# A two-layer hybrid decoder step on one core: new places for gate sums, first products and index writes, and a last norm taken token by token inside the loop

## The chip, the core and the metric

The program runs on one core of a Trainium2 chip. The engines are TensorE (PE), VectorE (DVE), ScalarE (ACT) and GpSimd (POOL); SyncE (SP) issues most DMAs and POOL the rest. The metric is the device time of one execution in microseconds; three runs of the kernel before gave 2693.7, 2697.02 and 2700.03 us, median 2697.02 us.

## What is computed

One inference step for a group of 256 prompt tokens (with 16 meta tokens ahead of them) and a group of 8 x 4 sample tokens, in all 320 columns with padding, of width 1024:

```python
for i in range(DEPTH):                      # 2 layers
    xn = rms_norm(h, norm_mix[i])
    h = h + (rwkv7_time_mix(xn, ...) if i % 2 == 0 else mamba2_mix(xn, ...))
    h = h + peer_ffn(rms_norm(h, norm_ffn[i]), w_q, sub_keys, u_tab, v_tab)
return rms_norm(h, norm_final), states...

def peer_ffn(xn, w_q, sub_keys, u_tab, v_tab):
    q = (xn @ w_q).reshape(T, 8, 2, 128)
    s = einsum('thzd,zhkd->thzk', q, sub_keys)          # two half-keys, 128 each
    sv, si = top_k(s, 16)
    top_s, pos = top_k(all 16 x 16 sums of sv, 16)      # 16 experts of 16384, per head
    gate = softmax(top_s)
    act = gelu(einsum('td,ted->te', x, u_tab[eidx]))
    return einsum('te,ted->td', gate * act, v_tab[eidx])
```

## The kernel before, in words

The residual `h` lies feature-major: 128 partitions, 8 blocks, 320 token columns. Four stages run one after the other: `rwkv` (0 to 427 us in the profiled execution), `peer` of layer 0 with three groups of 16 gathered tokens (to 1354 us), `mamba` (to 1753 us), `peer` of layer 1 with two groups (to 2675 us), and then `final`. Every stage opens tile pools in SBUF and PSUM and closes them at its end. The two `peer` stages are blocks of their own, whose order on each engine is a planner's: it goes by its own estimate of when things are ready, takes what was written first among what is ready, and leaves an instruction marked with `keep_in_program_order` behind everything that was written before it on its engine. The order on the chip is then fixed, and each engine works through it strictly.

**Products in three parts.** `load_w` (L288) fetches a 512 KB weight block into `wraw` (three buffers, SP), rounds it into `whi` (ACT, or POOL where told, L273/L275) and puts the rest into `wlo` (DVE L280 or POOL L278), two buffers each. `mm3` (L294) multiplies: eight pairs whi x xhi, whi x xlo, then eight wlo x xhi, 24 matmuls.

**The norm ahead of a stage.** `prenorm` (L320) makes `xh`, `xl` from h times the norm's weight without the mean square; `rmsnorm` (L304) takes squares on ACT, sums groups of four on DVE, and has PE sum over partitions (`psn`, L313); then square root (ACT L315) and reciprocal (DVE L316). The first products use the unnormed xh, xl, and their result is multiplied by the reciprocal (L876, L1281, L1313). `xn` (L318) is made besides.

**`peer` in its stages.** 16 query products (L869 on) and 96 score matmuls `pss` (L900). Then the U loop: 56 chunks b, in each of which a 512 KB block of the U table is split (low part on POOL, `leng=LP`) and multiplied with the tokens (`psc`, L299 to L302), with a gelu on ACT. DVE meanwhile does the two-level top-k of three token tiles (0: the samples, 1 and 2: the prompt halves), step by step from `topk`. At fixed chunks (`AFTER`, L1056) come the late parts: `gates` (L987: exp on ACT, its place kept, then sum, reciprocal and product on DVE) and, for tile 0, `indices` (L1001: two DVE instructions, six small writes to DRAM and three reads back, all DMAs issued by POOL) or, for tiles 1 and 2, `finish` (L993: three PE transposes `ptk`, place kept, then a copy to `sel`). Tile 1: gates at chunk 29, finish at 33; tile 2: 46 and 51; tile 0: 14 and 16.

Then the W loop: 64 groups of four tokens; one-hot rows are made on POOL, DVE and ACT and multiplied into per-token weights (L1101), with ten more U chunks between. Then the V loop: 128 chunks, each with 12 matmuls `acc` (L1202) on a split block of the V table; between them the remaining 62 U chunks and, in the background from chunk 20 to `G1`, the gathered rows of the 16-token groups (POOL indirect DMAs, DVE products L1124). At its end the four `acc` banks (two token halves, two feature halves) are copied, transposed back (L1221) and added to h (L1224). `h` itself is parked in DRAM (`hd`) and read back at chunk 122 (L1186), since its SBUF room serves as a buffer.

**`mamba`** projects 41 weight blocks (`proj`, L1256): first block 40 in `decays`, then the convolution blocks 32, 36, 16 and on. `NU` = 2 products use the unnormed input; ahead of the third, xh and xl are written again from `xn`. The products have two PSUM banks.

**`final`** (L1571) runs the feature-major rmsnorm on h and stores y in one DMA.

Of the kernel before, what the change touches and what calls it, by code (L numbers as in the profile page):

```python
# [23 lines left out]
F32 = mybir.dt.float32  # L24
# [143 lines left out]
def prep(I):  # L168
# [21 lines left out]
    A["vecs"] = v  # L190
    for g in _GROUPS:
        A[g] = pack_consts(g)
# [32 lines left out]
class K:  # L225
    def __init__(self, ctx, tc, a, o):
# [3 lines left out]
        self.pst = self.wr = None  # L230
# [27 lines left out]
    def psum(self, **tags):  # L258

        if self.pst is not None:  # L260
            self.pst.close()
        self.pst = ExitStack()
        self.ps = self.pst.enter_context(self.tc.tile_pool(name="ps", bufs=1, space=PSUM))
        self.pstags = tags
# [17 lines left out]
    def fetch(self, src, kb=8):  # L282
        raw = (self.wr or self.wp).tile([128, kb, 128], F32, name="wraw", tag="wraw", bufs=3)
        self.nc.sync.dma_start(raw, src)
        return raw
# [18 lines left out]
    def rmsnorm(self, out, h, g, sq, rp, tag="ps", rr=None):  # L304
# [3 lines left out]
        for k in range(KB):  # L308
            nc.scalar.activation(sq[:, k], h[:, k], AF.Square)
            if k % 4:  # L310
                nc.vector.tensor_add(sq[:, k], sq[:, k], sq[:, k - 1])
            if k % 4 == 3:
                nc.tensor.matmul(ps, lhsT=self.C["ones"], rhs=sq[:, k], start=k == 3, stop=k == KB - 1)  # L313
        r, ri = rr or (rp.tile([128, T], F32, name=n, tag=n) for n in ("rms", "rmsi"))
# [5 lines left out]
    def prenorm(self, out, h, g, xh, xl, sq, rr, tag):  # L320

        nc = self.nc
        for k in range(KB):
            nc.scalar.activation(xh[:, k], h[:, k], AF.Copy, scale=self.vec(g, k))
            nc.vector.scalar_tensor_tensor(xl[:, k], h[:, k], self.vec(g, k), xh[:, k].bitcast(F32), op0=ALU.mult, op1=ALU.subtract)
        self.rmsnorm(out, h, g, sq, None, tag, rr)
# [3 lines left out]
    def rwkv(self):  # L330
# [5 lines left out]
        self.wr = st.enter_context(tc.tile_pool(name="wr", bufs=3))  # L336
        st2 = ExitStack()
        bq = st2.enter_context(tc.tile_pool(name="q10", bufs=6))
        self.wp = st2.enter_context(tc.tile_pool(name="w", bufs=2))
# [140 lines left out]
        self.wp = st2.enter_context(tc.tile_pool(name="wn", bufs=2))  # L480
# [45 lines left out]
        def load_wo(n):  # L526
            for m in range(len(wt), n):
# [4 lines left out]
                else:  # L532
                    hi = self.wp.tile([128, KB, 128], F32R, name="whi", tag="whi", bufs=4)
                    lo = self.wp.tile([128, KB, 128], F32R, name="wlo", tag="wlo", bufs=4)
# [27 lines left out]
        self.wp = st2.enter_context(tc.tile_pool(name="wd", bufs=2))  # L562
# [17 lines left out]
        self.wr = None  # L580
# [249 lines left out]
    def peer(self, l, ng):  # L830
# [14 lines left out]
        gp = st.enter_context(tc.tile_pool(name="gp", bufs=1))  # L845
        self.wp = st.enter_context(tc.tile_pool(name="w", bufs=2))
        tp = st.enter_context(tc.tile_pool(name="tk", bufs=1))
# [6 lines left out]
        self.consts("cp", gp)  # L854
# [12 lines left out]
        ri = self.prenorm(xn, self.h, f"nf{l}", xh, xl, sq, (gview(60, (128, T)), gview(62, (128, T))), "m")  # L867

        qT = gview(20, (128, 16, T)); sk = gview(40, (128, 16, 128))  # L869
        for i in range(16):  # L870
            w = self.load_w(a[f"wq{l}"][i], heng=nc.gpsimd if i < LH else None, leng=8 if i < LQ else None)
# [4 lines left out]
            V.tensor_mul(qT[:, i], pq, ri)  # L876
# [33 lines left out]
        def topk(ti):  # L910
# [90 lines left out]
            def indices():  # L1001
# [3 lines left out]
                for i in range(3):  # L1005
                    dst = scr_i[i] if i < 2 else scr_g
                    src = ei[:, i] if i < 2 else fl(ts)
                    for hh in range(2):
                        x = nc.gpsimd.dma_start(dst[:, 64 * hh:64 * hh + 64], src[64 * hh:64 * hh + 64])
                        if i + hh == 0:  # L1010
                            tc.keep_in_program_order(x)
                    nc.gpsimd.dma_start(gi[:, i] if i < 2 else gg, dst[0:48].rearrange("(g t) (h m) -> (t h) g m", g=3, m=16))

            late[ti] = (gates, finish if ti else indices)
# [613 lines left out]
```

## Time and profile before

| | |
|---|---|
| three runs, median | 2697.02 us (2693.7 to 2700.03) |
| the profiled execution's own time | 2695.28 us |
| its span, first to last instruction | 2693.5 us |
| PE busy | 2500.8 us, 93% of the span |
| DVE, ACT, POOL busy | 1880.4, 1257.7, 1013.1 us |
| mean granted clock of TensorE | 0.968 |
| DMA | 460.28 MB, mean 171 GB/s |

PE is busy nearly throughout, so what is left to gain or lose lies in the stretches where it is not, and in those in which the granted clock is below 1.00. The profile is read stage by stage: first the busy time by stretch, then what PE waited for, then the instructions in order of time around each such wait.

### The profile page before, as it was taken

The page shows a single profiled execution, that of the slowest core. Times are in us where ns is not written, and L with a number is a line of the kernel's source. Part 1 is how long each engine was busy: PE and PEld are TensorE (multiplying, and loading weights), DVE is VectorE, ACT ScalarE, POOL GpSimd, SP SyncE. Part 2 cuts the span into 40 slices and gives each one's busy share as a digit, 9 for nine tenths or more (in the row PEclk, how much of TensorE's full clock was granted, in tenths as well). Part 3 has the DMA queues.
Part 4 walks back from the last instruction along what each step waited for, and adds up shares of the span by engine and source line. Part 5 has one row for each costly group of instructions (what it writes and reads, how often), then busy time and mean ns, then how long its engine had stood idle before and what let it go on. Part 6 is the DMA issues. An engine that isn't in the chain of part 4 may idle for free. (4 is left out here: it accounts for less than half of the span.)

```text
span 2693.5 us, 47369 instructions
## 1 busy us (share of the span) xinstructions
PE 2500.8 (93%) x18261; PEld 2168.8 (81%) x18261; DVE 1880.4 (70%) x3692; ACT 1257.7 (47%) x2337; POOL 1013.1 (38%) x896
## 2 busy tenths in 40 slices
PE   7999998978999999999969898989789899999997
PEld 4677768978988888888855786989789788888885
DVE  5355556795595677778783787759938856777776
ACT  3322223434784444444556543335347744444443
POOL 4111110468880232424156445006678601223120
PEclk9999999989999999999989999999899999999998
DMA  3111114434416788888732443354353267888774
GB/s 147 52 45 50 34 59 157 137 121 147 141 56 208 248 313 302 301 301 313 245 99 86 145 160 116 126 175 148 113 155 111 73 219 250 272 270 271 259 268 143
DMA packets 125154, 460.28 MB, mean 171 GB/s; under 512 B 14688, under 2 KB 15616, under 8 KB 121600
## 3 DMA queue, kind: packets, MB, share of 16 engines
q1 hardware_dynamic: 98784, 360.69, 41.4%
q0 software_dynamic: 26144, 96.56, 10.0%
q8 instruction: 144, 2.36, 0.4%
q14 instruction: 82, 0.67, 0.1%
HBM read 440.38 MB, written 16.82 MB: 170 GB/s over the span
## 5 line engine op out<-in xcount | busy, mean ns | idle before, releaser
L273 ACT CAST whi<-wraw 128x1024 fp32r<-128x1024 f32 (+1 forms) x619 | 643.2, 1039 | 890.9 <-PE acc L1202 243.0
L280 DVE TENSOR_TENSOR wlo<-wraw,whi 128x1024 fp32r<-128x1024 f32 (+1 forms) x493 | 598.3, 1214 | 369.9 <-ACT whi L273 345.3
L299 PE MATMUL psc<-xh,whi 128*128 128x256 f32 x2048 | 516.5, 287 | 2.0 <-ACT whi L273 2.0
L300 PE MATMUL psc<-xl,whi 128*128 128x256 f32 x2048 | 517.2, 287 | 0.0
L278 POOL TENSOR_TENSOR wlo<-wraw,whi 128x1024 fp32r<-128x1024 f32 (+1 forms) x150 | 356.7, 2385 | 194.6 <-PE pq L302 92.2
L299 PEld LDWEIGHTS psc<-xh,whi 128*128 128x128 f32 x2048 | 392.3, 192 | 8.5 <-ACT whi L273 3.7
L300 PEld LDWEIGHTS psc<-xl,whi 128*128 128x128 f32 x2048 | 392.0, 191 | 5.3
L302 PE MATMUL psc<-xh,wlo 128*128 128x256 f32 x2048 | 299.5, 286 | 34.5 <-POOL wlo L278 34.5
L302 PEld LDWEIGHTS psc<-xh,wlo 128*128 128x128 f32 x2048 | 269.2, 191 | 36.0 <-POOL wlo L278 35.4
L1202 PE MATMUL acc<-whi,glo 128*128 128x512 f32 x1024 | 279.4, 394 | 6.7 <-DVE glo L280 6.7
L1202 PE MATMUL acc<-whi,gh 128*128 128x512 f32 x1024 | 280.1, 394 | 4.3 <-ACT whi L273 3.3
L1032 POOL DMA_INDIRECT G<-in_un,gi x80 | 110.1, 1377 | 457.2 <-DVE glo L280 316.4
L1202 PE MATMUL acc<-wlo,gh 128*128 128x512 f32 x1024 | 276.5, 392 | 0.9 <-DVE wlo L280 0.9
L1202 PEld LDWEIGHTS acc<-whi,glo 128*128 128x128 f32 x1024 | 193.2, 189 | 51.0 <-DVE glo L280 7.6
L1202 PEld LDWEIGHTS acc<-wlo,gh 128*128 128x128 f32 x1024 | 192.8, 189 | 44.4 <-DVE wlo L280 2.2
L1129 POOL DMA_INDIRECT G<-in_v,gi x80 | 120.4, 1505 | 278.3 <-DVE G L1124 166.1
L1202 PEld LDWEIGHTS acc<-whi,gh 128*128 128x128 f32 x1024 | 184.0, 189 | 40.0 <-ACT whi L273 6.4
L1101 PE MATMUL pwt<-ob,oa 128*128 128x128 f32 x1024 | 145.3, 280 | 9.5 <-DVE ob L1075 6.1
L1101 PEld LDWEIGHTS pwt<-ob,oa 128*128 128x128 f32 x1024 | 128.9, 191 | 18.3 <-issue 14.3
L299 PE MATMUL pi<-xh,whi 128*128 128x320 f32 x328 | 107.7, 340 | 10.3 <-DVE cst L1281 7.4
L280 DVE TENSOR_TENSOR glo<-G,gh 128x256 fp32r<-128x256 f32 x256 | 107.0, 419 | 3.1 <-ACT gh L273 3.1
L1083 POOL TENSOR_SCALAR oa<-cp,sel 128x128 f32<-128x128 f32 x128 | 105.7, 835 | 7.5 <-issue 4.3
(469 smaller groups left out, 4453.9 us busy)
## 6 DMA issues: line engine op xcount, KB each, us to landing
wraw<-in_u SPq DMA_DIRECT2D x256, 512.0 KB, 3.9
wraw<-in_v SPq DMA_DIRECT2D x256, 512.0 KB, 4.4
wraw<-in_win SPq DMA_DIRECT2D x41, 512.0 KB, 3.7
wraw<-in_wq SPq DMA_DIRECT2D x32, 512.0 KB, 4.1
wraw<-in_rkv SPq DMA_DIRECT2D x24, 512.0 KB, 3.4
h<-in_ssm SPq DMA_DIRECT2D x8, 1024.0 KB, 7.9
out_sssm<-h POOLq DMA_DIRECT2D x8, 1024.0 KB, 5.3
wraw<-in_wo SPq DMA_DIRECT2D x8, 512.0 KB, 4.6
```

Of the source, the lines that this page charges most:

```text
L273: self.nc.scalar.copy(hi, x)
L278: self.nc.gpsimd.tensor_sub(lo[:, :n], x[:, :n], hi[:, :n].bitcast(F32))
L280: self.nc.vector.tensor_sub(lo[:, n:], x[:, n:], hi[:, n:].bitcast(F32))
L299: nc.tensor.matmul(ps, lhsT=whi[:, k], rhs=xhi[:, x0 + k], start=start and k == 0, stop=False)
L300: nc.tensor.matmul(ps, lhsT=whi[:, k], rhs=xlo[:, x0 + k], start=False, stop=False)
L302: nc.tensor.matmul(ps, lhsT=wlo[:, k], rhs=xhi[:, x0 + k], start=False, stop=stop and k == kb - 1)
L1032: nc.gpsimd.indirect_dma_start(out=rows, out_offset=None, in_=a[f"un{l}"], in_offset=bass.IndirectOffsetOnAxis(ap=gi[:, 0, g, m:m + 1], ax ...
L1083: nc.gpsimd.tensor_scalar(oa[:, j], C["iota"], sel[:, 0, t:t + 1], None, op0=ALU.is_equal)
L1101: mm(pw[:, j], lhsT=oa[:, j], rhs=ob[:, j], start=True, stop=True)
L1129: nc.gpsimd.indirect_dma_start(out=rows, out_offset=None, in_=vrows, in_offset=bass.IndirectOffsetOnAxis(ap=gi[:, 1, g, m:m + 1], axis=0))
L1202: mm(acc[i], lhsT=g[:, t0:t0 + 128], rhs=w[:, d0:d0 + 512], start=b == 0 and g is gh and w is vhf, stop=b == 127 and w is vlf)
```

## The change

Pools of `peer` and `mamba` and all PSUM pools are opened with `reuse_waits="tile"`: a tile in reused room waits for the tiles whose bytes it takes, and no longer for the whole pool that lay there. The weight pool (`wraw`, `whi`, `wlo`) is opened once for the whole program; the first three weights of a stage are fetched ahead of its constants. In `prenorm` the first product is written between the squares and their sum on PE. Query products alternate between two PSUM tags, and the first four mamba products have two banks each of two tags and are all unnormed. Of the late parts exp, gate sums and finish or indices have three places now; the DVE sum keeps its place; all nine index DMAs keep their place on POOL, six writes first, then three reads, after chunk 55. In the last layer h is transposed to token-major inside the V loop and the last norm is taken there token by token; `final` is gone and y has 288 rows.

```diff
-        self.ps = ...tile_pool(name="ps", bufs=1, space=PSUM)
+        self.ps = ...tile_pool(name="ps", bufs=1, space=PSUM, reuse_waits="tile")
+        self.wp = ctx.enter_context(tc.tile_pool(name="w", bufs=2))      # in K.__init__
...
     def rmsnorm(self, out, h, g, sq, rp, tag="ps", rr=None, mid=None):
...
-            if k % 4 == 3:
+            if k % 4 == 3 and mid is None:
                 nc.tensor.matmul(ps, lhsT=self.C["ones"], rhs=sq[:, k], ...)
+        if mid is not None:
+            mid()
+            for k in (3, 7):
+                self.tc.keep_in_program_order(
+                    nc.tensor.matmul(ps, lhsT=self.C["ones"], rhs=sq[:, k], ...))
...
# peer
+        raws = {i: self.fetch(a[f"wq{l}"][i]) for i in range(3)}
-        gp = st.enter_context(tc.tile_pool(name="gp", bufs=1))
+        gp = st.enter_context(tc.tile_pool(name="gp", bufs=1, reuse_waits="tile"))
...
-        self.consts("cp", gp)
+        with tc.issue_after(self.fetched):
+            self.consts("cp", gp)
...
-            pq = self.bank([128, T], "pq", "s")
+            pq = self.bank([128, T], "pq", "so"[i % 2])
...
+            def exps():
+                tc.keep_in_program_order(nc.scalar.activation(es, es, AF.Exp))
             def gates():
-                tc.keep_in_program_order(nc.scalar.activation(es, es, AF.Exp))
-                V.tensor_reduce(mxs, es, axis=AX.X, op=ALU.add)
+                tc.keep_in_program_order(V.tensor_reduce(mxs, es, axis=AX.X, op=ALU.add))
...
-        AFTER = ((14, 16), (29, 33), (46, 51))
+        AFTER = ((14, 16, 55), (29, 31, 39), (46, 46, 52))
...
# peer, last layer: in the gather generator, for the ng groups of 16 tokens
+            if last:
+                for half in range(2):
+                    ph = self.bank([128, 512], "ph", "s")
+                    for g in range(ng):
+                        for k in range(4):
+                            mm(ph[32 * g:32 * g + 16, ...], lhsT=self.h[:, 4 * half + k, 16 * g:16 * g + 16], rhs=C["eye"], ...)
+                    for g in range(ng):
+                        nc.scalar.copy(o, ph[32 * g:32 * g + 16])
+                        V.tensor_add(o, o, ga[half][32 * g:32 * g + 16])
...
+        def normed(z, ps, i, rows):
+            for half in range(2):
+                V.scalar_tensor_tensor(yt half, z half, 1.0, z half, op0=mult, op1=mult, accum_out=f[:, half:half + 1])
+            V.tensor_add(f[:, 2:3], f[:, 0:1], f[:, 1:2])
+            nc.scalar.activation(f[:, 2:3], f[:, 2:3], AF.Sqrt, bias=C["cst"][ps, 0:1], scale=1.0 / D)
+            V.reciprocal(f[:, 3:4], f[:, 2:3])
+            for half in range(2):
+                V.scalar_tensor_tensor(yt[:, c], z[:, c], f[:, 3:4], gfin[ps, c], op0=ALU.mult, op1=ALU.mult)
+                nc.sync.dma_start(self.o["y"][rows, c], yt[:, c])
...
-        G1 = 120
+        G1 = 124 if last else 120
...
-            if b == 122:
+            if b == (120 if last else 122):
                 nc.sync.dma_start(self.h, hd)
+            if b == 124 and last:                       # 16 transposes of h, 4 copies on ACT
...
+        if last:                                        # after the loop, instead of L1211 to L1224 and final
+            for i in range(2):
+                for half in range(2):
+                    V.tensor_add(ht[i] half, ht[i] half, acc[2 * i + half])
+                normed(ht[i], slice(0, 128), 2 + i, slice(32 + 128 * i, 160 + 128 * i))
...
# mamba
+        raws = {b: self.fetch(a["win"][b]) for b in (40, 32, 36)}
-        NU = 2
+        NU = 4
+        pre = {b: self.load_w(a["win"][b], leng=LE, raw=raws[b]) for b in (40, 32)}
...
-            p = self.bank([128, T], "pi", "i")
+            p = self.bank([128, T], "pi", "i" if done[0] % NU < 2 or done[0] >= NU else "f")
...
-    def final(self): ...
```

## Rows read from the trace of the kernel before

**Rows 1.** Busy time of each engine in three stretches: the start of peer 0, the start of mamba, the V loop of peer 1. Columns: length, then busy us and instructions of PE, weight loads, DVE, ACT, POOL, then the granted TensorE clock, the DMA share and GB/s.

```profile
420.00:470.00 50.00, 41.53 (x258) 39.75 (x258) 30.34 (x44) 16.56 (x27) 5.54 (x4) 0.90 0.54 177
...
1350.00:1400.00 50.00, 34.27 (x196) 30.78 (x194) 44.81 (x65) 30.55 (x63) 25.73 (x31) 0.86 0.36 115
...
2140.00:2672.00 532.00, 529.09 (x2988) 462.87 (x2988) 367.25 (x479) 254.33 (x378) 99.08 (x67) 0.99 0.76 250
```

**Rows 2.** The waits of PE over the whole span, the three longest in total: who waited, for whom, us in total, times, longest.

```profile
PE psc L302 <- POOL wlo L278: 34.5, 4, 13.3
PE psn L313 <- issue: 27.3, 4, 9.7
PE ptk L996 <- DVE G L991: 20.2, 2, 10.1
```

**Rows 3.** The timeline from the last product of rwkv to the scores of peer 0: start, us, engine, line, operation, count, idle time before it in brackets.

```profile
426.70 0.45 PE L302 MATMUL po<-oh,wlo 128*128 128x320 f32 x2
...
434.80 1.41 PE L313 MATMUL psn<-G,c 128*128 128x320 f32 x2 [7.64 <-issue]
...
489.28 1.34 PE L302 MATMUL pq<-xh,wlo 128*128 128x320 f32 x8
492.80 1.34 PE L302 MATMUL pq<-xh,wlo 128*128 128x320 f32 x8
...
497.50 3.73 PE L900 MATMUL pss<-G 128*128 128x128 f32 x32
```

**Rows 4.** The same from mamba to peer 1.

```profile
1749.99 0.69 DVE L280 TENSOR_TENSOR wlo<-wraw,whi 128x512 fp32r<-128x512 f32 x1
...
1752.32 0.75 PE L302 MATMUL pout<-hl,wlo 128*128 128x320 f32 x4
...
1825.40 3.73 PE L900 MATMUL pss<-G 128*128 128x128 f32 x32
```

**Rows 5.** The same from peer 0 to the third product of mamba.

```profile
1354.83 3.73 ACT L324 ACTIVATE xh<-h,vecs 128x320 fp32r<-128x320 f32 x8 [1.21 <-PE pot L1221]
...
1361.25 2.88 PE L313 MATMUL psn<-sq,c 128*128 128x320 f32 x4 [6.80 <-issue]
...
1379.17 0.61 PE L299 MATMUL pi<-xh,whi 128*128 128x320 f32 x1 [7.39 <-DVE cst L1281]
```

**Rows 6.** Busy time in stretches of the U loop and the W loop of peer 0, columns as in the first group.

```profile
560.00:570.00 10.00, 9.48 (x80) 9.27 (x78) 10.00 (x61) 2.99 (x6) 3.67 (x2) 1.00 0.36 130
570.00:580.00 10.00, 0.00 (x0) 0.00 (x0) 10.00 (x54) 0.00 (x0) 0.76 (x2) 0.67 0.00 1
580.00:590.00 10.00, 7.24 (x44) 7.24 (x45) 10.00 (x31) 2.86 (x4) 5.77 (x4) 0.64 0.36 111
590.00:600.00 10.00, 6.04 (x31) 5.83 (x31) 10.00 (x31) 2.48 (x3) 9.84 (x9) 0.70 0.36 112
630.00:640.00 10.00, 1.72 (x15) 1.47 (x13) 9.90 (x7) 2.66 (x4) 4.79 (x3) 0.75 0.54 159
...
710.00:720.00 10.00, 10.00 (x90) 10.00 (x89) 10.00 (x24) 9.13 (x29) 9.27 (x12) 1.00 0.35 107
```

**Rows 7.** POOL's timeline in the U loop of peer 0.

```profile
537.09 2.39 POOL L278 TENSOR_TENSOR wlo<-wraw,whi 128x1024 fp32r<-128x1024 f32 x1 [0.49 <-ACT whi L273]
539.97 2.43 POOL L278 TENSOR_TENSOR wlo<-wraw,whi 128x1024 fp32r<-128x1024 f32 x1 [0.49 <-ACT whi L273]
...
579.24 1.10 POOL L1009 DMA_DIRECT2D scr_g<-G  x2 [15.56 <-DVE G L945]
...
584.98 0.81 POOL L1012 DMA_DIRECT2D gg<-scr_g  x1
590.12 2.11 POOL L1009 DMA_DIRECT2D scr_i<-ei  x4 [4.34 <-DVE ei L1004]
...
596.87 1.56 POOL L1012 DMA_DIRECT2D gi<-scr_i  x2
```

**Rows 8.** DVE's timeline at the end of the top-k of peer 0.

```profile
611.30 3.41 DVE L984 TENSOR_TENSOR G<-G 128x2048 bf16<-128x2048 bf16 x1
...
637.50 1.22 DVE L984 TENSOR_TENSOR G<-G 128x2048 bf16<-128x2048 bf16 x1
...
640.97 0.28 DVE L989 TENSOR_REDUCE G<-G 128x8 f32<-128x128 f32 x1
...
641.51 0.29 DVE L991 TENSOR_TENSOR G<-G 128x128 f32<-128x128 f32 x1
```

**Rows 9.** The timeline of the V loop's end and of what follows it.

```profile
2601.35 1.28 DVE L1124 SCALAR_TENSOR_TENSOR G<-G,act 128x1024 f32<-128x1024 f32 x1
...
2671.01 1.07 PE L1202 MATMUL acc<-wlo,gh 128*128 128x512 f32 x4
2672.07 1.09 PE L1221 MATMUL pot<-c,G 128*128 128x128 f32 x8
...
2687.96 0.34 SPq L1579 DMA_DIRECT2D out_y<-y  x1
```

**Rows 10.** DMA issues: KB of each, median us from issue to landing.

```profile
wraw<-in_wout SPq DMA_DIRECT2D x16, 256.0 KB, 2.9
...
h<-hd SPq DMA_DIRECT2D x2, 1280.0 KB, 7.8
...
out_y<-y SPq DMA_DIRECT2D x1, 1280.0 KB, 4.5
```

More of the change, by code (lines that the diff above doesn't have):

```diff
@@ L190, in prep @@
     A["vecs"] = v
+    A["nfin"] = np.ascontiguousarray(I["norm_final"].reshape(1, D))
     for g in _GROUPS:
@@ L262, in psum @@
         self.pst = ExitStack()
-        self.ps = self.pst.enter_context(self.tc.tile_pool(name="ps", bufs=1, space=PSUM))
+        self.ps = self.pst.enter_context(self.tc.tile_pool(name="ps", bufs=1, space=PSUM, reuse_waits="tile"))
         self.pstags = tags
@@ L282, in fetch @@
     def fetch(self, src, kb=8):
-        raw = (self.wr or self.wp).tile([128, kb, 128], F32, name="wraw", tag="wraw", bufs=3)
-        self.nc.sync.dma_start(raw, src)
+        raw = self.wp.tile([128, kb, 128], F32, name="wraw", tag="wraw", bufs=3)
+        self.fetched = self.nc.sync.dma_start(raw, src).ins
         return raw
@@ L1008, in indices @@
                     for hh in range(2):
[L1009 to L1014, printed above, removed]
+                        tc.keep_in_program_order(nc.gpsimd.dma_start(dst[:, 64 * hh:64 * hh + 64], src[64 * hh:64 * hh + 64]))
+                for i in range(3):
+                    tc.keep_in_program_order(
+                        nc.gpsimd.dma_start(gi[:, i] if i < 2 else gg,
+                                            (scr_i[i] if i < 2 else scr_g)[0:48].rearrange("(g t) (h m) -> (t h) g m", g=3, m=16)))
+            late[ti] = (exps, gates, finish if ti else indices)
         late_u = []
@@ L1062, in peer @@
             for ti in range(3):
-                for i in range(2):
+                for i in range(3):
                     if b == AFTER[ti][i]:
@@ L1209, in peer @@
             pass
+        if last:
+            for i in range(2):
+                for half in range(2):
+                    V.tensor_add(ht[i][:, half * 512:half * 512 + 512], ht[i][:, half * 512:half * 512 + 512], acc[2 * i + half])
+                normed(ht[i], slice(0, 128), 2 + i, slice(32 + 128 * i, 160 + 128 * i))
+            st.close()
+            return
         for i, pt in enumerate(self.gpt):
@@ L1232, in mamba @@
         st = ExitStack()
-        pp = st.enter_context(tc.tile_pool(name="mp", bufs=1))
-        self.consts("cm", pp)
+        raws = {b: self.fetch(a["win"][b]) for b in (40, 32, 36)}
+        pp = st.enter_context(tc.tile_pool(name="mp", bufs=1, reuse_waits="tile"))
+        with tc.issue_after(self.fetched):
+            self.consts("cm", pp)
         xh = pp.tile([128, KB, T], F32R, name="xh")
@@ L1269, in proj @@
             return p
-        gp = st.enter_context(tc.tile_pool(name="mg", bufs=2))
+        first = []
+        ri = self.prenorm(xn, self.h, "nm1", xh, xl, ep.tile([128, KB, T], F32, name="sq", tag="E"), (rr[:, 0], rr[:, 1]), "t",
+                          lambda: first.append(proj(40)))
+        gp = st.enter_context(tc.tile_pool(name="mg", bufs=2, reuse_waits="tile"))
         def conv(blk):
```

109 lines of the change are left out of this document (66 added, 43 removed).

## The prediction

> **What bounds the kernel now.** I read the busy time by stretch first. The V loop runs PE at 529.1 of 532 us [rows 1], and the U and W loops come near it, so nothing is won where PE runs at 1.00; the first reading also shows the exceptions: at a stage's start PE stands for a tenth to a third of 50 us, at a granted clock of 0.90 or 0.86 [rows 1]. Then I read PE's waits: three kinds make 82 us [rows 2], and each comes once per boundary or once per peer layer. psn waits at stage starts; psc waits for POOL's low parts in the U loop; ptk waits for DVE's gates. The timeline around each says why. "issue" is the name for a wait whose releaser is not seen; at psn it is the chain h, xh, squares, sums. Last I read the 21.4 us behind the last acc matmul (2672.08 to 2693.5) [rows 9]: one chain with PE nearly idle.
>
> **The change part by part.** The sum stands against the profiled execution, 2695.3 us (span 2693.5 and 1.8 around it), 1.7 under the median of 2697.0.
>
> *rwkv to peer 0.* From the last product (427.15) to the scores (497.50) pass 70.3 us [rows 3]. The PE work in it at full clock: 16 products at 3.52 (492.80 less 489.28) make 56.3; four psn matmuls, 1.41 per two at the low level [rows 3], half of that at the high one: 1.4; eight transposes at 0.14 (1.09 for eight [rows 9]): 1.1. That is 58.8, so 11.5 is waiting (7.64 [rows 3]) and half-speed running after it. Removed: the wait of every new tile for the whole old pool, and psn's place ahead of the first product. The weights can be fetched and split by POOL while rwkv ends; xh and xl follow h block by block; only block 7 is left when PE ends, one piece each on DVE, ACT and DVE again of some 0.47 us (3.73 for eight [rows 5]), and the first 14 matmuls (2.1 us at 3.52 for 24) cover it. Late next: psn's second half needs eight squares on ACT, which at no more than 0.47 each end about 4.7 us after the last product, against 3.5 of the first product: 1 us. I take -10.5; bounds -11.5 and 0 (if a tile under xh is read to the end).
>
> *mamba to peer 1.* 1753.07 to 1825.40 is 72.3 [rows 4], 13.5 over the same 58.8. Here the weight buffers come free only with mamba's last splits (1749.99 [rows 4]), so the first low part may be 1 to 2 us late. -11.5; bounds -13.5 and 0.
>
> *peer 0 to mamba.* xh starts at 1354.83 right behind the transposed h [rows 5], and no pool holds it; that stays. The 6.80 ahead of psn shrinks, since the first product follows xl at 0.47 per block; the 7.39 ahead of the third product [rows 5] shrinks, since four products instead of two run before xh, xl are rewritten. PE alone would be 11 us earlier. But DVE, which makes xl twice, xn and the convolutions, is busy 44.8 of these 50 us [rows 1] and does the same work. Its 5.2 idle us are the nearest limit: -6; bounds -11 and 0. The three constants that now queue on SP behind the weights, the exp and the mask copy put in their place, and the changed banks cost nothing while ACT and SP have room here (ACT 30.6 of 50); without it 1 or 2 us.
>
> *U loops, twice.* A chunk takes 2.88 us (539.97 less 537.09 [rows 7]). At 579 POOL stands 15.56 us in front of a small write, waiting for tile 0's gates, and 4.34 at 590 [rows 7]; the low parts of the next chunks are queued behind it, and PE idles 17.2 of the 40 us from 560 (0.5, 10, 2.8, 4.0) and runs another 13.3 at a granted clock of 0.64 to 0.70 [rows 6], a mix of the 1.2 and the 2.4 GHz level, which costs some 4.4: about 22 us. At chunk 55 those gates have been ready for 100 us, so this goes. What is late next is tile 1's gate sum: it stands at the very end of DVE's order, behind all of tile 2's top-k (640.97, done 641.8 [rows 8]), and DVE is busy 10.00 of 10 up to there [rows 6]. Keeping the sum's place only forbids an earlier one, so I cost it at nothing. PE came to the old finish, chunk 33, 10.1 before that [rows 2], at 631.7; 22 earlier and six chunks on (17.3) it comes to the new one at 627, so PE waits there longer than before. And DVE will end later: the same operation takes 1.22 us with POOL quiet and 3.41 with POOL subtracting [rows 8]. Some eleven such operations ran in POOL's pauses; each now pays 0 to 2.2: I take 6 in all (the middle of a uniform start would be 12, but after one wait the next ones run in the gap), bounds 0 and 24. DVE's release comes at 648; 16 chunks are then left where 22 were: -17.3 + 6 = -11.
>
> The Trainium skill, "SBUF — State Buffer", section "Who interferes with whom", says that GpSimd and a VectorE operation on the shared port pair exclude each other for the whole instruction. Taken at its worst here, eleven whole subtracts (2.39 each [rows 7]), DVE would end 26 us later, each U loop would lose 9 instead of gaining 11, and the sum would be 2688; the row of 3.41 against 1.22 agrees with such blocking, though not that every operation meets it. That time is a rival of its own, at 0.04.
>
> Moved: the six writes and three reads, 1.10 + 0.81 + 2.11 + 1.56 = 5.6 us of POOL [rows 7], now stand between the last U chunk's low part and the W loop's one-hots, where POOL is busy 9.3 of 10 [rows 6]; the reads wait besides for their writes. Queued behind them: the half low part of chunk 56 and the one-hots, for which PE waits; three one-hot groups made ahead cover about 3 us. +4; bounds 0 and +8. The gathers want the indices only at V chunk 20. Per layer -7, twice -14.
>
> *The last norm.* Now 21.4 us follow the last matmul. Then: four adds, four squares, four scalings on DVE at 0.64 (half of the 1.28 for 1024 columns [rows 9]) make 7.7, small steps 0.6 (some 0.3 each [rows 8]), with the first add 0.4 before the last matmul's end: 7.9. Then issue 0.35, landing of 256 KB 2.9 [rows 10], and the 1.0 that followed the old landing (4.5 after 2687.96 [rows 9, 10], to 2693.5): 12.1, so -9.3. Added to the loop, in which PE has no room [rows 1]: 32 small matmuls at 0.14 less eight small transposes, +3.4. DVE gets some eight 0.64 us pieces in the last four chunks, where it is busy 69% (367 of 532 [rows 1]), 0.85 us free per chunk: about 1 us reaches PE (0 to 4). The h read goes two chunks earlier; 7.8 us to landing [rows 10] is three chunks, just its lead, and the V blocks behind it on SP live on three buffers; late, it costs one chunk. Sum -5; bounds -9 and +1.
>
> Sum: -10.5 - 11.5 - 6 - 14 - 5 = -47, so **2648 us**.
>
> **The rivals.** *No second wait.* If tile 1's sum comes to DVE before tile 2's top-k, finish finds its gates ready, and the 21 us of waiting and 1.5 of cold restart go as well, twice: 2603. For it: the sum misses by little, and the planner sees other times now. Against: exp stays at chunk 29, and DVE shows no idle time to pull anything into. 0.17.
>
> *The boundaries stay mostly shut.* If the overlapped tiles are just those read last, or ACT and POOL take the early casts late, a quarter of the 28 us is left: 2669; with none of it, so that the pools' edit does not do what it says, 2676. For it: psn's wait is put down to no releaser, so the trace does not name the tile; at mamba's start h itself is late. 0.16.
>
> *Slower: DVE's chain.* All the U loop's end hangs on tile 1's gates. Every microsecond by which DVE ends later passes to both layers once PE waits there. The gains are used up when DVE ends 23.5 us after my 648, that is some 30 after 641.8; at 675 the time is 2702. For it: DVE is full and POOL no longer pauses [rows 6, 7]. Against: while PE waits, POOL gets no buffers and stops subtracting (4.79 of 10 busy at 630 [rows 6]), so DVE then runs free. 0.04.
>
> **How the numbers follow.** The forecast has 0.58, its terms' bounds taken together about 2625 to 2672; the four rivals above have 0.41, unnamed orders of the planner 0.01. The range goes down to the first rival and up past the second: 2602 to 2678. A measurement of this kernel can tell about 0.2% from no change, 5.4 us. Faster by more: the forecast, no second wait, nearly all of the shut boundaries and half of the 2688: 0.90; the same 0.04; slower 0.06.
>
> **What would show it.** Right: no PE wait over 2 us at psn in peer 0 and peer 1, and their scores 10 to 12 us after the stage's start sooner; no psc wait for POOL near chunk 20; the wait at ptk of 15 to 25 us, at chunk 39, with the sum still DVE's last of the top-k; POOL's nine DMAs together after chunk 55 and PE gaps of a few us there; some 12 us behind the last acc matmul. Wrong: ptk without a wait (first rival), a wait of 5 us or more ahead of the first query product (second), a gate sum done later than 30 us after where it was against the scores (third), or PE standing in the last four V chunks.

## The result, and the profile after

The kernel after takes 2679.33 us (median of ten runs, 2676.22 to 2690.53) against 2695.86 for the kernel before beside it: ratio 0.9943, 95% interval 0.9931 to 0.9954, a gain of 16.5 us. I forecast 2648 and 2602 to 2678: the direction held, the size did not. The two profiled executions differ by 19.1 us of span (2693.5 and 2674.4). Cut at the same events, the span splits like this:

| stretch | before | after | forecast | found |
|---|---|---|---|---|
| rwkv, to its last product | 427.2 | 425.5 | 0 | -1.7 |
| to the scores of peer 0 | 70.3 | 62.6 | -10.5 | -7.7 |
| U and W loop, peer 0 | 310.8 | 308.3 | -7 | -2.5 |
| V loop, peer 0 | 542.1 | 546.6 | 0 | +4.4 |
| its end and mamba | 401.4 | 398.2 | -6 | -3.2 |
| to the scores of peer 1 | 72.3 | 66.8 | -11.5 | -5.5 |
| U and W loop, peer 1 | 310.8 | 305.0 | -7 | -5.8 |
| V loop of peer 1, last norm, store | 556.0 | 559.1 | -5 | +3.1 |

(The same rwkv code took 425.4 to 433.3 us in the profiles of this study, so its row means nothing. The U and W rows are cut 1.2 us short, here and below, in every kernel alike.) Against the sum of my terms 28 us are missing in these rows: 12.5 in the V loops, which got longer, 11.6 in the two starts and mamba, which opened by less than forecast, and 5.7 in the U and W loops, which gave 8 instead of 14; 1.7 of rwkv go the other way.

PE's waits, longest first, answer to [rows 2]: the long waits at psn in the peer stages and POOL's at psc are gone, and ptk has gone from 20.2 to 46.8 us, split over its three transposes.

```profile
PE ptk L1014 <- DVE G L1009: 20.5, 2, 10.2
PE ptk L1014 <- DVE G L1001: 18.7, 2, 9.4
...
PE ptk L1014 <- DVE G L1002: 7.6, 2, 4.6
PE psn L318 <- DVE sq L316: 7.5, 2, 7.4
```

Stretches of 10 us (and of the V loop), columns as in [rows 1]. The start of peer 0 runs at a granted clock of 1.00 at once, that of peer 1 at 0.71; while PE waits in the U loop (630 to 640), POOL does nothing at all.

```profile
435.00:445.00 10.00, 10.00 (x67) 9.65 (x66) 7.32 (x10) 3.58 (x4) 0.00 (x0) 1.00 0.61 211
...
630.00:640.00 10.00, 0.21 (x1) 0.00 (x0) 9.97 (x11) 0.00 (x0) 0.00 (x0) 0.50 0.00 0
...
690.00:700.00 10.00, 10.00 (x86) 9.88 (x86) 9.26 (x17) 6.98 (x18) 9.90 (x12) 1.00 0.41 123
...
1742.00:1752.00 10.00, 6.64 (x26) 5.67 (x25) 9.31 (x14) 4.68 (x12) 3.72 (x2) 0.71 0.85 285
...
2118.00:2631.00 513.00, 509.44 (x2875) 442.83 (x2876) 350.30 (x460) 241.80 (x359) 98.48 (x66) 0.99 0.77 254
```

The timeline at the two peer starts, answering to [rows 3, 4]: the first product follows 0.67 us behind the old stage's last; at peer 1 it then stands for DVE's xl, and its products come every 0.27 us (1752.42 to 1752.68) instead of 0.15. DVE makes all eight xl behind the last h: they begin 0.44 us behind the old stage's last product, in the kernel before 0.68.

```profile
425.94 3.79 DVE L336 SCALAR_TENSOR_TENSOR xl<-h,vecs,xh 128x320 fp32r<-128x320 f32 x8
426.17 0.39 PE L302 MATMUL pq<-xh,whi 128*128 128x320 f32 x1 [0.67 <-DVE h L586]
...
434.10 2.62 PE L305 MATMUL pq<-xh,wlo 128*128 128x320 f32 x16 [1.57 <-DVE wlo L283]
...
436.56 1.24 PE L323 MATMUL psn<-G,c 128*128 128x320 f32 x4
...
488.06 1.16 PE L916 MATMUL pss<-G 128*128 128x128 f32 x9
...
1742.78 6.67 DVE L336 SCALAR_TENSOR_TENSOR xl<-h,vecs,xh 128x320 fp32r<-128x320 f32 x8
1743.01 0.38 PE L302 MATMUL pq<-xh,whi 128*128 128x320 f32 x1 [0.67 <-DVE h L1641]
...
1744.62 0.42 PE L303 MATMUL pq<-xl,whi 128*128 128x320 f32 x1 [0.68 <-DVE xl L336]
...
1747.19 0.63 PE L303 MATMUL pq<-xl,whi 128*128 128x320 f32 x1 [2.00 <-DVE xl L336]
...
1752.42 0.47 PE L302 MATMUL pq<-xh,whi 128*128 128x320 f32 x1
1752.68 0.47 PE L303 MATMUL pq<-xl,whi 128*128 128x320 f32 x1
...
1809.09 1.16 PE L916 MATMUL pss<-G 128*128 128x128 f32 x9
```

The U loop of peer 0, answering to [rows 7, 8]: the transposes at chunk 39, DVE's gate sum and product of tile 1, and two of the lines of POOL's nine DMAs, which now stand around one-hots (oa).

```profile
619.90 0.47 PE L1014 MATMUL ptk<-c,G 128*128 128x128 f32 x1 [4.57 <-DVE G L1002]
629.74 0.47 PE L1014 MATMUL ptk<-c,G 128*128 128x128 f32 x1 [9.36 <-DVE G L1001]
640.44 0.47 PE L1014 MATMUL ptk<-c,G 128*128 128x128 f32 x1 [10.23 <-DVE G L1009]
...
637.18 0.28 DVE L1007 TENSOR_REDUCE G<-G 128x8 f32<-128x128 f32 x1
...
640.10 0.28 DVE L1009 TENSOR_TENSOR G<-G 128x128 f32<-128x128 f32 x1
...
687.12 2.20 POOL L1027 DMA_DIRECT2D scr_i<-ei  x4
...
693.33 0.83 POOL L1030 DMA_DIRECT2D gi<-scr_i  x1
```

The end, answering to [rows 9, 10]: 10.8 us from the last acc product (its group ends at 2663.6) to 2674.4; ahead of it ph and ga stand between the products.

```profile
2631.33 1.05 PE L1169 MATMUL ph<-c,h 128*16 128x128 f32 x8
2632.31 1.21 PE L1273 MATMUL acc<-whi,gh 128*128 128x512 f32 x4
...
2640.52 1.89 PE L1159 MATMUL ga<-G,cp 128*16 128x512 f32 x4
...
2662.50 1.10 PE L1273 MATMUL acc<-wlo,gh 128*128 128x512 f32 x4
2662.94 2.48 DVE L1284 TENSOR_TENSOR G<-G,acc 128x512 f32<-128x512 f32 x4 [0.64 <-PE acc L1273]
...
2668.56 2.72 DVE L1208 SCALAR_TENSOR_TENSOR G<-G,fin 128x512 f32<-128x512 f32 x4
```

And what the forecast had no line for: the same acc products, in the same loop, at a granted clock of 1.00. First the kernel before: the groups of four start 0.91 us apart.

```profile
2207.54 1.07 PE L1202 MATMUL acc<-whi,gh 128*128 128x512 f32 x4
2208.45 1.07 PE L1202 MATMUL acc<-whi,glo 128*128 128x512 f32 x4
2209.35 1.07 PE L1202 MATMUL acc<-wlo,gh 128*128 128x512 f32 x4
```

The kernel after: 0.93 to 0.94.

```profile
2186.22 1.09 PE L1273 MATMUL acc<-whi,gh 128*128 128x512 f32 x4
2187.16 1.10 PE L1273 MATMUL acc<-whi,glo 128*128 128x512 f32 x4
2188.09 1.09 PE L1273 MATMUL acc<-wlo,gh 128*128 128x512 f32 x4
```

Averaged from 2200 to 2250 us, two acc products in a row start 228.7 ns apart before, 233.5 after; psc goes the other way, 120.3 to 119.3. (Peer 0's V loop, taken whole, has 230.0 and 234.4 for acc.) Over 1536 acc and 1488 psc products that is 7.4 less 1.5, some 5.9 us per V loop. No instruction or operand shape differs there. What differs is where the tiles lie: the weight pool, opened once and early, starts at another byte of each partition.

### The profile page after: what moved, and what is told of

It is laid out like the page before. It is cut to its first block, busy times and chain, and to the rows that moved or that the text cites. A ratio compares the mean times of both kernels' runs of the same rounds, so it can differ in the third digit from the quotient of the medians.

```text
span 2674.4 us, 47364 instructions
## 1 busy us (share of the span) xinstructions
PE 2506.7 (94%) x18281; PEld 2156.3 (81%) x18281; DVE 1912.9 (72%) x3713; ACT 1246.7 (47%) x2324; POOL 1012.7 (38%) x895
## 5 line engine op out<-in xcount | busy, mean ns | idle before, releaser
L302 PE MATMUL psc<-xh,whi 128*128 128x256 f32 x2048 | 509.0, 285 | 4.6 <-ACT h L1065 2.6
L303 PE MATMUL psc<-xl,whi 128*128 128x256 f32 x2048 | 507.0, 284 | 0.0
L305 PE MATMUL psc<-xh,wlo 128*128 128x256 f32 x2048 | 291.6, 284 | 0.3 <-POOL wlo L281 0.3
L1120 PE MATMUL pwt<-ob,oa 128*128 128x128 f32 x1024 | 144.7, 281 | 11.6 <-DVE ob L1094 8.0
L303 PE MATMUL pi<-xl,whi 128*128 128x320 f32 x328 | 105.8, 334 | 4.1 <-DVE xl L336 3.8
```

The lines of the kernel that those rows point to most:

```text
L302: nc.tensor.matmul(ps, lhsT=whi[:, k], rhs=xhi[:, x0 + k], start=start and k == 0, stop=False)
L303: nc.tensor.matmul(ps, lhsT=whi[:, k], rhs=xlo[:, x0 + k], start=False, stop=False)
L305: nc.tensor.matmul(ps, lhsT=wlo[:, k], rhs=xhi[:, x0 + k], start=False, stop=stop and k == kb - 1)
L1120: mm(pw[:, j], lhsT=oa[:, j], rhs=ob[:, j], start=True, stop=True)
```

## The experiments

Intervals of the profiled executions, in us (before: 70.3, 310.8, 542.1, 401.4, 72.3, 310.8, 556.0). "Time" is the median, the ratio is to the kernel before on the same chip.

| kernel | start 0 | U+W 0 | V 0 | mamba | start 1 | U+W 1 | V 1 to end | time | ratio, interval |
|---|---|---|---|---|---|---|---|---|---|
| after | 62.6 | 308.3 | 546.6 | 398.2 | 66.8 | 305.0 | 559.1 | 2679.33 | 0.9943 (0.9931, 0.9954) |
| e1 weights at 64 | 62.7 | 306.8 | 540.5 | 399.3 | 66.6 | 307.6 | 550.0 | 2664.59 | 0.9891 (0.9858, 0.9924) |
| e2 finish at 52 | 62.5 | 293.2 | 545.5 | 400.6 | 67.5 | 289.1 | 557.2 | 2646.91 | 0.9811 (0.9789, 0.9833) |
| e3 old end | 62.4 | 307.3 | 544.8 | 401.0 | 66.4 | 305.2 | 563.8 | 2686.51 | 0.9960 (0.9943, 0.9978) |
| e4 pool waits | 64.3 | 309.2 | 545.5 | 400.3 | 67.4 | 307.2 | 558.9 | 2677.77 | 0.9924 (0.9904, 0.9944) |
| e5 all at 64 | 62.4 | 308.0 | 546.5 | 401.9 | 66.2 | 305.1 | 553.1 | 2668.92 | 0.9895 (0.9873, 0.9917) |
| e6 low on DVE | 62.6 | 308.5 | 543.0 | 399.1 | 67.0 | 306.3 | 557.7 | 2678.42 | 0.9943 (0.9926, 0.9961) |
| e7 no fetch | 62.7 | 307.4 | 549.0 | 403.8 | 66.8 | 304.9 | 557.9 | 2683.30 | 0.9954 (0.9941, 0.9967) |
| e8 psn first | 66.2 | 307.8 | 547.0 | 403.4 | 68.7 | 306.3 | 558.3 | 2685.93 | 0.9965 (0.9950, 0.9981) |
| e9 before, plus 32 | 70.5 | 309.6 | 543.7 | 405.0 | 72.2 | 312.5 | 559.2 | 2703.94 | 1.0022 (1.0010, 1.0034) |
| e10 x at 64 | 62.5 | 304.4 | 538.6 | 400.2 | 66.8 | 309.3 | 553.3 | 2672.73 | 0.9911 (0.9889, 0.9933) |
| e11 indices at 40 | 62.6 | 306.7 | 546.1 | 401.4 | 67.1 | 303.8 | 557.8 | 2674.30 | 0.9920 (0.9896, 0.9944) |
| e12 both | 62.7 | 287.2 | 542.4 | 399.3 | 66.9 | 286.2 | 550.0 | 2626.12 | 0.9734 (0.9709, 0.9758) |
| e13 pool alone | 69.7 | 308.6 | 544.2 | 402.5 | 70.4 | 305.4 | 559.7 | 2687.41 | 0.9978 (0.9966, 0.9990) |

Stretches of unchanged code scatter from profile to profile: the first start by 0.3 us (62.4 to 62.7 in nine kernels that leave it alone), the second by 1.3, the U and W loops by some 4, mamba by 3.7, the V loop by up to 6. So a single row shows little under these sizes, and the distances between instructions show more. The kernel before took 2693.0 to 2697.4 us on the chips of these runs; a difference of two medians can be off by that, and the ratio takes it out.

**Where the weights lie: e1, e9, e5, e10.** The edit of e1:

```diff
+        ctx.enter_context(tc.tile_pool(name="pad0", bufs=1)).tile([128, 8], F32, name="pad0")
         self.wp = ctx.enter_context(tc.tile_pool(name="w", bufs=2))
+        ctx.enter_context(tc.tile_pool(name="pad1", bufs=1)).tile([128, 8], F32, name="pad1")
```

> Kernel after with 32 unused bytes ahead of the weight pool and 32 behind it. The weight pool's tiles move from byte 41312 of a partition (32 past a multiple of 64) to 41344 (a multiple of 64); G, xh, gh keep their remainder to 64. In the V loops the acc products follow each other every 233.4 ns in the kernel after, every 228.6 in the kernel before, where the pool lay at 197376, a multiple of 64. Theory 'remainder': the 4.8 ns per product come from the 32 bytes; then 228.6 or less comes back here, each V loop is 1536 x 4.8 = 7.4 us shorter less about 1.5 that psc won (119.3 against 120.3 ns), so some 12 us in all: 2667. Rival 'region': the cost comes from how far the weights lie from gh or from the rest; then nothing changes: 2679, products at 233.4. Rival 'not the address': the same 2679.

The V loops got 6.1 and 9.1 us shorter, the time 14.7 us (14 by the ratios, with an interval of some 9 either way). In e1 the groups of four are back at 0.91:

```profile
2201.74 1.07 PE L1275 MATMUL acc<-whi,glo 128*128 128x512 f32 x4
2202.65 1.08 PE L1275 MATMUL acc<-wlo,gh 128*128 128x512 f32 x4
2203.56 1.08 PE L1275 MATMUL acc<-whi,gh 128*128 128x512 f32 x4
```

e9 puts the same two pads around the weight pool of the kernel before:

> Kernel before with 32 unused bytes ahead of the weight pool of its peer stages and 32 behind it: weights go from 197376 (a multiple of 64) to 197408 (32 over), xh stays 32 over, gh stays at a multiple of 64. It is e1 turned round, at the other end of the memory. Theory 'remainder of the streamed weights': acc goes from 228.6 to 233.4 ns, each V loop from 542.1 and 534.7 us to some 548 and 540; 2697 + 11 = 2708. Rival 'where in the memory': at 197408 nothing changes: 2697, 228.6 ns.

The kernel before became slower by 32 bytes, with groups of four 0.93 apart:

```profile
2203.74 1.09 PE L1204 MATMUL acc<-whi,glo 128*128 128x512 f32 x4
2204.67 1.09 PE L1204 MATMUL acc<-wlo,gh 128*128 128x512 f32 x4
2205.60 1.09 PE L1204 MATMUL acc<-whi,gh 128*128 128x512 f32 x4
```

acc went where expected; the time rose by less (0.22%, 6 us by the ratio, not 11), since psc won 2.5 ns per product at the same time: 6.3 us more less 3.7, per V loop.

e5 has one pad ahead of the weights and one ahead of gh's pool (`tk`), e10 one behind the weights and one ahead of gh's pool:

> Kernel after with 32 unused bytes ahead of the weight pool and 32 ahead of the pool of gh: weights, G and the tokens xh, xl of the peer stages now all lie at multiples of 64 (in e1 xh, xl kept 32 over); mamba's xh, xl go the other way, from 0 to 32 over. Theory 'whatever PE streams': psc, which streams xh and xl, gains as acc did in e1 (233.4 to 229.5 ns, 1.7%): 117.0 to 115.0 ns, 6144 products in two layers, 12 us below e1: 2652, less the few us that mamba's pi loses. Rival 'the stationary side': in e1 psc gained (119.3 to 117.0) when only its stationary operand moved; then xh's place changes nothing: 2665 as e1. Rival 'weights pool alone, because DMA writes it': the same 2665.

> Kernel after with xh, xl and G moved to multiples of 64 and the weights left 32 over: the fourth corner to after, e1 and e5. acc should stay at 233.4 ns and the V loops near 546 and 548 us, since acc streams the weights. For psc, which streams xh and xl (119.3 ns in after, 117.0 in e1 with only the weights moved, 119.9 in e5 with both): if equal remainders of weights and tokens decide, psc comes out like e1, near 117; if the tokens' own remainder decides, near 119.9. Time 2675 to 2680 either way.

All six kernels together, ns between starts in one 50 us stretch of peer 1's V loop:

| | before | e9 | after | e1 | e5 | e10 |
|---|---|---|---|---|---|---|
| weights past a multiple of 64 | 0 | 32 | 32 | 0 | 0 | 32 |
| tokens xh, xl past it | 32 | 32 | 32 | 32 | 0 | 0 |
| acc (streams weights) | 228.7 | 232.8 | 233.5 | 229.5 | 229.2 | 232.8 |
| psc (streams tokens) | 120.3 | 117.8 | 119.3 | 117.0 | 119.9 | 116.8 |

acc follows the weights' remainder in all six. Both good places of the weights (41344 and 197376) are multiples of 128 too, so these runs do not tell 64 from 128; and why TensorE takes longer is not shown. psc follows none of the three theories: among the four kernels built on after it is fast where the remainders differ; of before and e9 it is fast in e9, where they are equal. Which relation of the two places counts for psc stays open. The V loop's length follows less strictly than these distances: in e5 peer 0's shows no gain (546.5), since PE waited there 5.9 us for ACT's whi (1.6 in after), and in e10 it is the shortest of all (538.6) with slow acc, a fast psc and 0.5 us of that wait.

**The wait at ptk: e2 and e12.** The edit of e2, then of e12 (which has e1's pads too):

```diff
-        AFTER = ((14, 16, 55), (29, 31, 39), (46, 46, 52))
+        AFTER = ((14, 16, 55), (29, 31, 52), (46, 46, 53))
...
+        AFTER = ((14, 16, 53), (29, 31, 53), (46, 46, 55))
```

> Kernel after with the transposes and copy of tile 1 behind chunk 52 and of tile 2 behind chunk 53 (39 and 52 in the kernel after). Theory: the second wait is nothing but the place of these transposes; DVE's chain ends at 640 us however long PE waits, and PE has chunks to do meanwhile. Then the 26.9 and 25.1 us that chunk 40 takes above 2.88 go, and the 1.9 behind them, in both layers: 54 us less, some 2626. DVE pays for a POOL that no longer pauses, some 5 to 10 us, which chunk 52 (at 651 us) just covers. Rival: DVE's chain stretches by over 12 us, a new wait of 5 to 10 us stands at chunk 52 or 53 in each layer: 2636 to 2646. Rival: the one-hots of the W loop, which start when the copy is done, come late, and the W loop gives back 10 us a layer: 2646.

A gain of 32 us (36 by the ratios), not 54. PE's long wait is gone, but DVE's chain, and with it a smaller wait, moved back. DVE in the kernel after, with POOL idle:

```profile
626.14 1.21 DVE L1000 TENSOR_TENSOR G<-G 128x2048 bf16<-128x2048 bf16 x1
627.27 0.21 DVE L982 CAST G<-G 128x128 f32<-128x128 uint32 x1
627.41 2.27 DVE L1001 TENSOR_REDUCE G<-G 128x128 f32<-128x2048 bf16 x1
```

The same three in e2, with POOL subtracting, and the transposes at the end of the chain:

```profile
629.91 3.43 DVE L1000 TENSOR_TENSOR G<-G 128x2048 bf16<-128x2048 bf16 x1
633.26 2.44 DVE L982 CAST G<-G 128x128 f32<-128x128 uint32 x1
635.62 2.27 DVE L1001 TENSOR_REDUCE G<-G 128x128 f32<-128x2048 bf16 x1
...
658.65 0.33 PE L1014 MATMUL ptk<-c,G 128*128 128x128 f32 x1 [2.59 <-DVE G L1009]
...
667.08 0.47 PE L1014 MATMUL ptk<-c,G 128*128 128x128 f32 x1 [2.47 <-DVE G L1009]
```

The two-input operation and the cast pay 2.2 each, nearly the length of a subtract (2.4 [rows 7]); the reduction pays nothing. From the scores to tile 1's gates DVE takes 144.3 us before (497.5 to 641.8), 152.3 after, 168.8 in e2: the less PE waits, the less POOL pauses, the longer DVE's chain. Summed over that chain, the same 65 two-input operations (TENSOR_TENSOR) take 65.6 us before, 72.9 after and 88.7 in e2, while the search operations stay as they are (120 MAX8: 29.7, 29.3 and 29.1). So the wait had been buying DVE 16.5 us. My expectation had 5 to 10; its first rival (over 12 us, a new wait of 5 to 10, 2636 to 2646) came out at its upper edge. The other rival, late one-hots, did not: from the first product of the one-hots (pwt) to the first acc pass 111.7 us in e2, 115.9 after. The Trainium skill, "SBUF — State Buffer", section "Who interferes with whom", has this pattern (a two-input VectorE operation in conflict with GpSimd's reads, tensor_reduce never on trn2), and these rows agree.

> Kernel after with the weights at multiples of 64 (as e1) and the last parts of all tiles later: tile 0's DMAs and tile 1's transposes behind chunk 53, tile 2's behind 55. e1 took 14.7 us off, e2 32; in e2 PE still waited 4.6 and 6.4 us (layer 0) and 7.7 (layer 1) at the transposes, because DVE's chain, with a POOL that never pauses, ended at 658.5 instead of 640.4. Theory: the two add up, and the later place takes some 8 us of those waits, with POOL's DMAs under one of them: 2679 - 15 - 32 - 8 = 2624. Rival: nothing is left between the last transposes and the W loop, and what PE doesn't wait at the transposes it waits at the first one-hots: 2632.

2626.12, 2.7% under the kernel before and 2.0% under the kernel after: the gains add. Without the later place e1 and e2 add up to 2632, the rival's time; the 6 us below it are no more than the interval, 13 us wide, leaves open. The wait of peer 0 is down to one of 6.1 us at ptk, and peer 1 has none there.

**The last norm: e3.** The edit puts back the end of the kernel before:

```diff
-        G1 = 124 if last else 120
+        G1 = 120
-            if b == (120 if last else 122):
+            if b == 122:
...
+        k.final()
```

> Kernel after with the end of the kernel before: gathered rows to G1 = 120 and back to feature-major, h read at chunk 122, the four banks transposed back, feature-major norm, one store of y. Theory: the token-major norm shortens what follows the last acc product from 21.4 to 10.8 us (10.6), and costs 8 us of PE in the last eight chunks (16 small products of two passes, 16 transposes, the switches between them), where I had counted 3.4 and 1: so it is worth 2 to 3 us in all, and this kernel takes 2682. Rival: the V loop's last chunks are slow for another reason (the weights' place, the h read); then the loop stays long and the time rises by the whole 10.6: 2690.

From the V loop's start to the end 563.8 against 559.1: the new norm is worth 4.7 us by the rows, 7 by the medians, 4.6 by the ratios. That is between theory and rival: the last eight chunks take 23.6 instead of 32.2, the tail 22.1 instead of 10.8, and the loop ahead of them 518.1 instead of 516.1, since with G1 = 120 the products of ga (1.9 us) fall into it.

**The W loop: e11.**

```diff
-        AFTER = ((14, 16, 55), (29, 31, 39), (46, 46, 52))
+        AFTER = ((14, 16, 40), (29, 31, 39), (46, 46, 52))
```

> Kernel after with tile 0's six writes and three reads behind chunk 40 instead of 55. Theory: what the W loop gave back (from chunk 55 to its end 4.9 us more in each layer than before) is POOL's time for these nine DMAs; at chunk 40 PE stands at the transposes of tile 1 and POOL is idle for over 20 us, so there they are free: chunk 56 comes 2.8 us sooner, the W loop 4 to 5, in each layer: 2671. Rival: DVE bounds the W loop (it is busy 10 of 10 from 720 to 780), and the end of it doesn't move: 2679; or the low part of chunk 41 waits behind the nine and PE loses the 5.6 there: 2679.

From the 55th U chunk (54, counted from 0) to the V loop the time fell from 114.6 to 109.5 us in both layers, as the theory has it; but the U loops took 3.5 and 3.9 us more, because the six writes stood ahead of chunk 40's subtract (tile 1's gates came at 643.1, not 640.4) and the reads still came after the wait. By the intervals 1.6 and 1.2 us are left, which the scatter hides; the medians' 5 us lie within their intervals. The place of the DMAs is shown to cost the W loop its 5 us; a gain from moving them to chunk 40 is not shown.

**The starts: e4, e7, e8, e13, e6.** e4, e7, e8 and e6 in this order; e13 has the edits of e4, e7 and e8 at once.

```diff
-        gp = st.enter_context(tc.tile_pool(name="gp", bufs=1, reuse_waits="tile"))      # e4, and all other pools
+        gp = st.enter_context(tc.tile_pool(name="gp", bufs=1))
...
-        raws = {i: self.fetch(a[f"wq{l}"][i]) for i in range(3)}      # e7, and raws, pre in mamba
+        raws = {}
...
-                          lambda: pq.append(query(0)))      # e8, and in mamba
+                          None)
...
-    leng=8 if i < LQ else None,      # e6
+    leng=8 if i < LQ and l == 0 else None,
```

> Kernel after with every pool opened without waits by tile: a stage's new tiles wait again for the whole pool that lay there. Weights are still fetched ahead, the first product still stands ahead of psn. Theory: it is the pool's wait that shut the stage starts; the intervals from a stage's last product to its scores go from 62.6 and 66.8 us back towards 70.3 and 72.3, mamba's start loses 3 or more: 2679 + 7.7 + 5.5 + 3.3 = 2695 or a little less, since the weights stay fetched. Rival: the gain at the starts comes from the weights fetched ahead and the order of the first product; then this kernel stays at 2679 to 2682.

Wrong in the main: of the 7.7 and 5.5 us 1.7 and 0.6 come back (64.3 and 67.4), the first beyond its scatter, the second not; the time does not move. At peer 0 all eight xh stand behind the old stage's last product again, the first 0.09 us behind it, as in the kernel before, and the squares come 2.7 us later than after; but the first weight was rounded 5.25 us ahead of that product.

> Kernel after without fetching three weights ahead of a stage's constants (peer and mamba) and without splitting mamba's first two ahead; the first product still stands ahead of psn. Theory: after e4 the pools are out; what opened the starts is the weights that are there when the last product ends. Then the first product waits for its weights, 3 us of landing and 4 us of POOL's cast and subtract at each start: 2679 + 5 + 5 + 3 = 2692. Rival: the place of the first product alone opened them: 2679 to 2682, and the intervals stay at 62.6, 66.8.

Wrong for the peer stages (62.7, 66.8), and there the edit did not do what I meant: at peer 0 POOL still rounded the first weight 4.7 us ahead of the old stage's last product (5.0 after), so this run says nothing of weights that come late. Mamba takes 403.8, 5.6 over after and 1.9 over the longest of the nine kernels that leave its start alone.

> Kernel after with psn written ahead of the first product again (peer and mamba); weights still fetched ahead. Theory: PE, which works in its written order there, stands at psn until the eight squares and their sums are made, some 5 to 8 us at each peer start at which no product can run: the intervals go from 62.6 and 66.8 to 68 to 72; 2679 + 6 + 4 + 3 = 2692. Rival: the weights fetched ahead alone opened the starts, the planner puts the first product ahead of psn by itself: 2679.

Right in kind: PE stands at psn again, and 3.6 and 1.9 us return at the peer starts, 5.2 in mamba (with a scatter of 3.7).

```profile
433.06 1.41 PE L318 MATMUL psn<-G,c 128*128 128x320 f32 x2 [5.96 <-DVE G L316]
```

> Kernel after with all three openings of the stage starts undone at once: waits by tile (e4), weights fetched ahead (e7) and the first product ahead of psn (e8); the weight pool that is opened once for the program stays. Alone, undoing them lengthened the starts of peer 0, peer 1 and mamba with its body by 1.7, 0.6 and 2.1 us (e4), 0.1, 0.0 and 5.6 (e7), 3.6, 1.9 and 5.2 (e8). Theory 'each can stand in for another': together they bring back the whole difference to the kernel before: peer starts of 70.3 and 72.3 us, mamba at 401 to 406; 2679 + 17 = 2696. Rival 'the weight pool does the rest': the starts stay at the sum of the single ones, 67.9 and 69.3; 2679 + 12 = 2691.

69.7 and 70.4: at peer 0 7.1 of the 7.7 are back, 1.7 more than the single ones add up to (5.4). The wait is once more one without a releaser, as in [rows 3]:

```profile
440.08 1.41 PE L318 MATMUL psn<-G,c 128*128 128x320 f32 x2 [9.74 <-issue]
```

So at peer 0 the three make nearly all of the gain. The rows show which stand in for one another: waits by tile and the early fetch, since with either of them the first weight is rounded ahead of the last product, and with neither 4.26 us behind it (before: 4.79). The squares come 2.7 us later besides, as in e4, and PE stands at psn for 9.74 us instead of e8's 5.96. What e13 keeps, the weight pool and the second PSUM tag of the query products, gives 0.6 at most. At peer 1 1.9 of 5.5 stay; which of the two gives them is not shown. The time (2687.41; the profiled execution took 2694.9) returned by 8 us, not 17.

> Kernel after with the low part of the first query block of peer 1 alone on DVE instead of POOL (peer 0 unchanged, as a control). At peer 1 DVE's eight xl took 6.67 us (0.83 each) while POOL cast and subtracted from 1743.1 to 1746.8; at peer 0, where POOL was done before, 3.79 us (0.47 each). Theory: POOL's subtract stops DVE's xl, the 2.9 us go from DVE to PE, and without it the interval from mamba's last product to the scores goes from 66.8 us towards 62.6, less the 1.22 of the subtract now on DVE: 64 to 65; total 2677. Rival: the slow xl waits for something else (the squares on ACT, the half clock of PE): then 66.8 stays or grows to 68: 2680.

At peer 1 one xl of the kernel after took 2642 ns, the median 540 (group of xl from 1742 to 1752: count, then min, median and max):

```profile
L336 DVE SCALAR_TENSOR_TENSOR xl<-h,vecs,xh x8: 539/540/2642, 1742.8 to 1748.9; 128x320 fp32r<-128x320 f32 x8
```

Without POOL's subtract the eight took 4.63 us instead of 6.67, but PE then waited for DVE to make the low part:

```profile
1741.95 4.63 DVE L336 SCALAR_TENSOR_TENSOR xl<-h,vecs,xh 128x320 fp32r<-128x320 f32 x8
...
1749.77 2.50 PE L305 MATMUL pq<-xh,wlo 128*128 128x320 f32 x8 [2.35 <-DVE wlo L283]
```

That POOL's subtract holds up xl is shown, a gain is not: the interval is 67.0. DVE, 9.31 of 10 us busy in after and 9.14 in e6, probably bounds this start whichever engine subtracts.

## Why the prediction was wrong

- **The first step that failed is one that had no term.** The V loops were costed at nothing but the norm's extra products, with the sentence that PE runs at 1.00 there and nothing is won. Nothing was won, but 4.8 ns per acc product were lost, some 5.9 us per loop, because the program-wide weight pool starts 32 bytes past a multiple of 64. e1 and e9 show it in both directions. Twice 5.9 are some 12 of the 28 us between the forecast and the profiled execution; the 14.7 of e1 hold besides what psc gains there and had not lost.
- **The starts: mechanism half right, sum too large.** I had -28, found -16.4. I named the pools' wait and psn's place; e4 shows the pools' edit worth 1.7 and 0.6 us while the early fetch stays, e8 the first product's place worth the most. The step that failed is "xh and xl follow h block by block; only block 7 is left": xh did follow (seven of the eight began 3.0 us or more ahead of the end of the old stage's last product, in the kernel before none), xl did not. DVE began the first xl 0.44 us behind the old stage's last product, hardly sooner than the 0.68 of the kernel before, although it stood idle for 3.03 us just ahead of the last h. So at peer 0 the first eight pairs of products came at the pace of xl, every 0.46 us and not every 0.29 (426.17 to 430.03). That is 1.5 us, nearly the whole difference between my 58.8 and the 60.4 that are left of 62.6 without the waits of 0.67 and 1.57. Whether DVE's order or a tile still in use held xl back is not shown. At peer 1, where POOL's subtract stretched xl besides, the clock, which I took as restored, fell to the low level behind waits of 0.68 and 2.00 us and stayed there until 1753. And mamba kept 3.2 of 6, a size that its scatter of 3.7 leaves uncertain: PE's waits ahead of psn and of the products pi did not shrink, 17.1 us before and 17.5 after, but fell into nine pieces instead of four. Most of them are now put down to ACT, which waits for DVE in turn (6.2 us at xc, 5.2 at x); DVE is busy 47.0 of the 50 us from 1345.
- **U loops: right wait, right size.** Forecast a wait of 15 to 25 us at ptk; found 24.2 in peer 0 (4.57 + 9.36 + 10.23). I added 6 to DVE's chain for a POOL that pauses less; the chain grew by 8.0. W gave back 4.9, against 4, and e11 shows POOL's DMAs behind it. With 1.5 us more for the chunk behind the wait (4.35 instead of 2.88: PE did not stand there, but the granted clock was at the low level until 643.7), peer 0's U and W loops came out 4.5 short of the forecast; in peer 1 1.2. The scatter of some 4 leaves the difference between the layers open.
- **Last norm: right in the sum, with some luck.** -5 forecast, -4.7 by e3. Against e3 the tail got 11.3 us shorter where I had 9.3, and the loop 6.6 longer where I had 4.4; the two misses cancel.
- **The rivals.** "Mostly shut" is nearest in time (2676 with none of the starts) but not the cause. "No second wait" would hardly have given 2603: e2 and e12 took PE's wait away, if by another way, and DVE's chain grew by 16.5 us and more. The rule of blocked ports, which I gave 0.04 as a time, was the right mechanism at a smaller dose: 8.0 us more than before with POOL pausing, 24.5 more when it does not pause, where I had 26 as the worst.

## What to carry to other kernels

When an edit moves a pool, look at where every streamed tile lands: compare the start-to-start distance of unchanged matmuls in the two traces first, since here 2% of a saturated loop was more than most of the scheduling edits gave. An engine that waits may be what lets another run free, so before removing a wait, cost the chain behind it with the engines that will no longer pause. And where several edits open the same door, undo them together as well as singly before saying which one did it.

## What the hardware showed that I had not expected

A 128x512 product of TensorE came 228.7 to 229.5 ns behind the last where its streamed weights lay at a multiple of 64 bytes, 232.8 to 233.5 where they lay 32 past it, six kernels out of six, at a granted clock of 1.00 (whether 64 or 128 is the step, they do not tell). At peer 1's start the granted clock was 0.71 over 10 us and the products ran at the low level (0.27 us apart) from behind the last of three waits, of 0.67, 0.68 and 2.00 us, until 1753; at peer 0's, after 0.67 and later 1.57 us, it stayed at 1.00.
